# Holding every instruction behind the first group of products in the source's order on its engine

## The chip, the cores and the metric

The kernel runs on one core of a Trainium2 chip. The metric is the time of one execution on the device in microseconds (us), as the median of several runs.

## The reference: one layer of a hybrid decoder

The reference computes one inference step of one layer with three kinds of heads side by side: 6 mLSTM heads (A), 6 gated delta-rule heads (B) and 4 HGRN2 heads (C), each 128 wide. A prompt of 1024 tokens, with 16 learned meta tokens in front, and 8 short sequences of 8 tokens go through the same weights. Cut to what matters:

```python
h = _rmsnorm(x, norm_w)
proj = jnp.einsum('bld,de->ble', h, w_in)          # one combined projection, D_MODEL 2048
(aq, ak, av, ao, ai, af, bq, bk, bv, ba, bb, cq, cf, ci, z) = jnp.split(proj, SPLIT_POINTS, axis=-1)
...
for ls in seg_lens:                                 # the meta tokens, then the prompt
    o, st_a = _mlstm_segment(...)                   # gated linear attention with a running maximum
    o, st_b = _gdn_segment(...)                     # per chunk a triangular system is solved
    o, st_c = _hgrn_segment(...)                    # per-dimension decay
hcat = hcat * lax.rsqrt(jnp.mean(hcat * hcat, axis=-1, keepdims=True) + EPS)
y = hcat.reshape(bsz, L, MIX) * out_norm_w.astype(f32) * jax.nn.silu(z.astype(f32))
out = jnp.einsum('ble,ed->bld', y.astype(x.dtype), w_out)
return x + out, (st_a[0], st_a[1], st_a[2], st_b, new_conv, st_c)
```

A last RMS norm over `x + out` gives `y_prompt` and `y_sample`; the states of the heads after the prompt and after each short sequence are outputs too. All is in 32 bits.

## The kernel before

**Halves, heads and pieces.** The tokens are worked in two halves: the first holds the short sequences (64 columns), the meta tokens (16) and half of the prompt (512 columns), the second the other 512. In each half the columns of the combined projection are computed head by head, in groups; a head needs four or five tiles of 128 columns (`k`, `q`, `v`, `o`, `z` for A, `k`, `q`, `v`, `z` for B, `f`, `q`, `v`, `z` for C). Behind the second half comes the output projection, in units of 512 output columns: four units with five blocks of tokens each for the first half (the last four blocks are prompt rows, the first the short sequences), then five units for the second. An accumulator is a PSUM bank (`acc`, in the output `oacc`); there are eight banks in all, for these and for everything else that TensorE writes.

**The feed.** The projections go in 32 bits at full matmul speed by splitting: a weight piece of 512 rows by 128 columns, `wraw`, is loaded by a DMA on SP's queue; ScalarE makes its rounded high part `whi`, VectorE the rest `wlo = wraw - whi`; TensorE then multiplies high by high, high by low and low by high. Each of the three has four buffers. While TensorE works on piece p, `feed_ahead` splits piece p+3 and then issues the load of piece p+7. A piece has 24 products of 288 or 304 columns in the first half and 12 of 512 in the second.

**Scans beside the products.** The work of a head behind its tiles (its scan) is written as a Python generator; each `yield` ends a step. Four queues hold such generators: `scan`, `fin` (the norm and gate of a head's output, `finish`), `post` and `bg`. Behind each four or so products `weave.pump()` looks at the head of each queue and issues its next step, if the step is due. What is due comes from a model of the program itself: `Clock` keeps a time for each of TensorE, VectorE, ScalarE and GpSimd, adds a cost for each instruction that is issued, and a step's follower is due `LATENCY = 0.4` us behind the end of the last instruction of the step; a few steps add a hint of their own (`ck.last += 8.0` behind the substitution, `ck.last += 2.5` behind the loads of an A head). Each instruction goes through `Engine.__getattr__` (line 137 issues it, so nearly every compute instruction has that line in the profile); each DMA goes through `DMA`, SP's queue. At most two heads are open: `start_head` drains the older one, and at the units of the output `weave.drain_queue` drains a queue to its end.

**The order on the engines.** The program thus issues all instructions in one sequence, the source's order. Before this change that is only a priority: the build orders each engine's queue itself, and where by its own estimate an instruction's operands or buffers are not ready, a later one of the same engine that is ready goes ahead. The order so found is fixed at build time; the engine then runs its queue from front to back.

Names used below:

- A heads, `mlstm_scan`: `turn_in` loads the values (`v1`) and the output gate (`og`) in turned layout; then the gate of the 80 small rows (transpose `pot`, ScalarE's `t<-pot`), the gate of the prompt rows (`S.activation(og, og, ...)` twice, `s<-s` in the profile), and in the first half `meta_rows`, a ScalarE copy of the 16 meta rows (`meta`), which the product `pum` reads.
- B heads, `gdn_scan`: `Ball` is written out to DRAM (`db`) and read back as rows `Bb`; `substitute` solves blocks of 16 rows in 15 steps of two VectorE operations, `Yt<-Yc,Bb` and `Yc<-Yc,Yt`, then a product with a mask into `Y2` and a transpose into `X2` (`Y` and `X` in the profile), which the products `pz` read.
- C heads, `hgrn_scan`: seven levels, each with exponentials `Ex` on ScalarE, sums on VectorE, products `X` on GpSimd, and then scores `pa` on TensorE.
- `prep_B` (queue `bg`, begun in group 19 of the first half) prepares the second half's input: loads `px`, squares (`pxs`), transposes, and writes `hbhi` and `hblo`, which `load_hB` reads into `hB` when the second half starts.
- At the end of each output unit, for each block of tokens: a DMA loads the residual rows `res`, VectorE adds the accumulator to them (which frees the bank), ScalarE squares them (`oscr`), GpSimd multiplies by the last norm's weights `fnw`. At the end of the first unit the queues `scan` and `fin` are drained and four loads of `fnw` are issued before that. `finish` writes a turned copy (`yd`) to DRAM, loads it back (`s<-yd`), gates it and stores its high and low parts (`y<-zs`, `y<-y`), which `load_y` reads for the output products.

Of the kernel before, what the change touches and what calls it, by code (L numbers as in the profile page):

```python
# [48 lines left out]
class Half:  # L49
    def __init__(self, index):  # L50
        self.index = index
        self.first = index == 0
        self.width = WA if self.first else WB
        n0 = 1 if self.first else 0

        self.base = NT0 if self.first else 0
        self.tiles = ([(HALF, NT0)] if self.first else []) + [(P * c, P) for c in range(NC)]
        self.gtiles = ([(0, NT0)] if self.first else []) + [(self.base + P * c, P) for c in range(NC)]
        self.groups = ([Group(NT0, 1, HALF, 0, True)] if self.first else []) + [Group(P, NC, 0, n0, False)]
        self.ggroups = ([Group(NT0, 1, 0, 0, True)] if self.first else []) + [Group(P, NC, self.base, n0, False)]  # L60
        self.main, self.gmain = self.groups[-1], self.ggroups[-1]
# [24 lines left out]
class Clock:  # L86


    def __init__(self):
        self.t = {"T": 0.0, "V": 0.0, "S": 0.0, "G": 0.0}  # L90
        self.dep = self.last = 0.0

    def begin(self):
        self.dep = self.last = self.t["T"]
# [14 lines left out]
class Engine:  # L109
# [21 lines left out]
    def __getattr__(self, op):  # L131
        f = getattr(self.engine, op)

        def call(out, *a, **k):
            fast = self.name == "T" and op == "matmul" and a[0].dtype == F32R
            self.clock.run(self.name, self.cost(op, out, fast) + (1.2 if k.get("op") == ALU.pow else 0.0))
            return f(out, *a, **k)  # L137
        return call


class Stream:
    def __init__(self, gen, lag=None):
        self.gen, self.lag, self.due, self.done = gen, lag, 0.0, False

# [46 lines left out]
def hybrid_step(ctx, tc, i, o):  # L191
    nc = tc.nc
    ck = Clock()
    V, S, G, T = (Engine(ck, n, e) for n, e in (("V", nc.vector), ("S", nc.scalar), ("G", nc.gpsimd), ("T", nc.tensor)))
    DMA = nc.sync.dma_start
    weave = Weave(ck)

    cp = ctx.enter_context(tc.tile_pool(name="cp", bufs=1))
# [31 lines left out]
    def w_raw(col, g):  # L230
        raw = wp.tile([P, 512], F32, tag="wraw", name="wraw")
        v = raw.rearrange("p (k c) -> p k c", c=P)
        if col is None:
            V.memset(raw, 0.0)
            for src, at in ((C_AI, 0), (C_BB, 32), (C_AF, 64), (C_BA, 96)):
                DMA(v[:, :, at:at + HA], i["w_in"][0, 512 * g:512 * (g + 1), src:src + HA].rearrange("(k p) c -> p k c", p=P))
        else:
            DMA(v, i["w_in"][0, 512 * g:512 * (g + 1), col:col + P].rearrange("(k p) c -> p k c", p=P))
        return raw

    def o_raw(k, cg):
        raw = wp.tile([P, 512], F32, tag="wraw", name="wraw")
        DMA(raw, i["w_out"][0, P * k:P * (k + 1), 512 * cg:512 * (cg + 1)])
        return raw
# [49 lines left out]
    def run_group(half, cols, accs, parts, after=None):  # L294
        for g in range(NG):
            for n in range(len(cols)):
                whi, wlo = next_piece()
                for q in range(4):
                    k = 4 * g + q
                    cs = slice(P * q, P * (q + 1))  # L300
                    products = [(whi, 0, k == 0, False), (whi, 1, False, False), (wlo, 0, False, k == NK - 1)]
                    if cols[n] is None:
                        products = [(whi, 0, k == 0, False), (whi, 1, False, k == NK - 1)]
                    for w, part, first, last in products:
                        for a, off, cnt in accs[n][parts]:
                            T.matmul(a[:, 0:cnt], w[:, cs], hT[g][part][:, q, off:off + cnt], start=first, stop=last)
                    if q == 1:
                        feed_ahead()
                    weave.pump()
            if after:  # L310
                after(g)
# [50 lines left out]
    def load_nw(tile_, g):  # L362
        DMA(tile_, i["norm_w"][0:1, 512 * g:512 * (g + 1)].partition_broadcast(P))
        return tile_
# [4 lines left out]
    def load_x(n):  # L369
        xs = [row(("eghj" if n in (3, 4) else "abcd")[g], f"x{g}")[:, 0:512] for g in range(NG)]  # L370
        for g in range(NG):
            cs = slice(512 * g, 512 * (g + 1))
            if n:
                DMA(xs[g], i["x_prompt"][0, P * (n - 1):P * n, cs])
            else:
                DMA(xs[g][0:NSAMP], xs_flat[:, cs])
                DMA(xs[g][NSAMP:NT0], i["meta_tokens"][:, cs])
# [80 lines left out]
    first_accs = new_accs(halves[0], group_lists[0][0])  # L458
    run_group(halves[0], first_cols, first_accs, slice(0, 1))
    weave.drain_queue("bg")  # L460


    params = cp.tile([P, 92], F32, name="params")
# [1278 lines left out]
    for half in halves:  # L1742
        toks = []
        for n, (c0, cnt) in enumerate(half.tiles):
            if half.first and n == 0:
                toks.append((0, NSAMP, xs_flat, ys_flat))
            else:
                a = HALF * half.index + c0
# [85 lines left out]
```

## Time and profile before

| what | value |
|---|---|
| median of 3 runs | 2505.61 us (2505.42 to 2511.15) |
| profiled execution, its own time | 2506.0 us |
| its span | 2504.3 us |
| granted TensorE clock | 0.990 |
| instructions in the span | 43941 |
| TensorE busy | 2442.1 us, 98% |
| VectorE busy | 1425.5 us, 57% |
| ScalarE busy | 991.2 us, 40% |
| GpSimd busy | 554.8 us, 22% |
| moved by DMA | 350.82 MB, mean 140 GB/s |

The span runs from the first to the last instruction; the time of the execution has 1.7 us around it. In rows of the profile an instruction stands as output<-inputs by the program's names without numbers, so several tiles with one tag can share a name (`s`, `t`, `y`). PE is TensorE, PEld its weight loads, DVE is VectorE, ACT ScalarE, POOL GpSimd, and SPq the queue of DMA issues on SP. A row of the time line has the start, the duration, the engine, the line, the operation, output<-inputs, and in brackets the idle time of the engine before it with what ended it.

### The profile page before, as it was taken

Reading aid. Unit: us, or ns where it says so; the run is one execution under the profiler, and the core shown is the slowest. Engines: PE = TensorE matmul, PEld = TensorE weight load, DVE = VectorE, ACT = ScalarE, POOL = GpSimd, SP = SyncE. Lnnn points to the kernel's source line nnn. Section 1 sums busy time; section 2 is a strip of 40 time slices with the busy share of each in tenths; the row PEclk is TensorE's granted clock in tenths of the full one; section 3 lists DMA queues with packets and bytes.
Section 4 is the critical chain, followed back from the end, with each engine's and each line's share of the span. In section 5 each row is a group of like instructions: output and inputs, shape, how many; then the busy total and the mean of one; then the engine's idle time right before and its main releaser. Section 6 shows DMA issues by size and latency. Waiting matters only on the chain.

```text
span 2504.3 us, 43941 instructions
## 1 busy us (share of the span) xinstructions
PE 2442.1 (98%) x16032; PEld 2184.5 (87%) x16032; DVE 1425.5 (57%) x3080; ACT 991.2 (40%) x2430; POOL 554.8 (22%) x743
## 2 busy tenths in 40 slices
PE   6999999999999999999999999999999999999998
PEld 5898999999999999999787888888888888888886
DVE  7775655765656655556864556554654545323435
ACT  5643434443435333333642434333443334222324
POOL 5331212420313312113320113110320102211201
PEclk9999999999999999999999999999999999999999
DMA  5656665655645454447554455454554558636735
GB/s 129 152 140 147 147 146 133 162 131 130 158 99 138 99 131 118 118 119 203 132 132 115 120 123 136 122 130 101 138 127 114 129 123 257 183 84 200 254 97 185
DMA packets 681045, 350.82 MB, mean 140 GB/s; under 512 B 260004, under 2 KB 622076, under 8 KB 680828
## 3 DMA queue, kind: packets, MB, share of 16 engines
q1 hardware_dynamic: 680828, 348.01, 54.3%
q8 instruction: 126, 2.06, 0.4%
q14 instruction: 91, 0.75, 0.1%
HBM read 285.71 MB, written 62.19 MB: 139 GB/s over the span
## 4 chain that ended last, share of the span: by engine, by line
PE 80%; issue 5%; DVE 5%; DMA 4%; ACT 2%; POOL 2%; SPq 1%; POOLq 0%; DVEq 0%; ACTq 0%
PE acc L137 59%; PE oacc L137 9%; PE pa L137 1%; DVE wlo L137 1%; PE po L137 1%; PE nd L137 1%; PE pz L137 1%; PE pyy L137 1%; DMA wraw<-in_w_in_dram 1%; POOL res L137 1%; PE pu L137 1%; DMA px<-in_x_prompt_dram 1%; ACT whi L137 1%; PE poh L137 1%; PE pw L137 1%
## 5 line engine op out<-in xcount | busy, mean ns | idle before, releaser
L137 DVE TENSOR_TENSOR wlo<-wraw,whi 128x512 fp32r<-128x512 f32 x720 | 525.6, 734 | 569.6 <-ACT whi L137 552.1
L137 PE MATMUL acc<-hA,whi 128*128 128x288 f32 (+1 forms) x4544 | 826.2, 304 | 11.3 <-ACT whi L137 6.4
L137 ACT CAST whi<-wraw 128x512 fp32r<-128x512 f32 x720 | 441.9, 618 | 929.1 <-PE acc L137 641.2
L137 PE MATMUL acc<-hB,whi 128*128 128x512 f32 x2272 | 722.2, 400 | 4.3 <-ACT whi L137 2.1
L137 PEld LDWEIGHTS acc<-hA,whi 128*128 128x128 f32 x4544 | 679.6, 191 | 18.2 <-ACT whi L137 8.1
L137 PE MATMUL acc<-hA,wlo 128*128 128x288 f32 x2240 | 489.7, 299 | 1.6 <-DVE wlo L137 1.6
L137 PEld LDWEIGHTS acc<-hB,whi 128*128 128x128 f32 x2272 | 413.6, 189 | 86.2 <-ACT whi L137 2.7
L137 PE MATMUL acc<-hB,wlo 128*128 128x512 f32 x1120 | 441.1, 394 | 2.6 <-DVE wlo L137 2.6
L137 PEld LDWEIGHTS acc<-hA,wlo 128*128 128x128 f32 x2240 | 367.7, 190 | 2.7 <-DVE wlo L137 2.6
L137 PE MATMUL oacc<-whi,y 128*128 128x512 f32 x1088 | 343.4, 390 | 1.1 <-ACT whi L137 1.1
L137 PEld LDWEIGHTS acc<-hB,wlo 128*128 128x128 f32 x1120 | 211.0, 188 | 52.0 <-DVE wlo L137 6.8
L137 PEld LDWEIGHTS oacc<-whi,y 128*128 128x128 f32 x1088 | 204.2, 188 | 44.5 <-ACT whi L137 2.4
L137 PE MATMUL oacc<-wlo,y 128*128 128x512 f32 x576 | 224.8, 390 | 1.2 <-DVE wlo L137 1.2
L137 PEld LDWEIGHTS oacc<-wlo,y 128*128 128x128 f32 x576 | 108.1, 188 | 25.2 <-DVE wlo L137 3.1
L137 POOL TENSOR_TENSOR res<-res,fnw 128x512 f32<-128x512 f32 (+1 forms) x34 | 54.3, 1627 | 255.4 <-ACT oscr L137 255.4
L137 POOL TENSOR_TENSOR y<-y,zs 128x592 fp32r<-128x592 f32 (+1 forms) x32 | 46.0, 1437 | 171.4 <-ACT zs L137 106.7
L137 POOL TENSOR_TENSOR qd<-qT,emb 128x512 f32<-128x512 f32 x12 | 17.7, 1479 | 230.3 <-PE po L137 230.3
L137 DVE TENSOR_TENSOR Yt<-Yc,Bb 128x60 f32<-128x60 f32 (+8 forms) x180 | 37.6, 209 | 43.9 <-DMA Bb<-db 39.0
L137 POOL TENSOR_TENSOR hr<-hr,halfneg 128x4 f32<-128x4 f32 (+1 forms) x48 | 44.1, 919 | 61.1 <-DVE hr L137 58.4
L137 POOL TENSOR_TENSOR nrm<-nrm,halfneg 128x10 f32<-128x10 f32 x12 | 23.5, 1960 | 138.9 <-DVE nrm L137 138.9
L137 POOL TENSOR_TENSOR X<-Ex,hk 128x256 f32<-128x256 f32 (+1 forms) x40 | 39.1, 978 | 63.2 <-PE pa L137 41.8
L137 ACT ACTIVATE Wt<-pw,nrm 128x128 f32<-128x128 f32 (+1 forms) x54 | 19.8, 367 | 78.1 <-PE pw L137 78.1
(416 smaller groups left out, 2766.7 us busy)
## 6 DMA issues: line engine op xcount, KB each, us to landing
wraw<-in_w_in_dram SPq DMA_DIRECT2D x564, 256.0 KB
wraw<-in_w_out_dram SPq DMA_DIRECT2D x144, 256.0 KB
y<-y SPq DMA_DIRECT2D x16, 576.0 KB
px<-in_x_prompt_dram SPq DMA_DIRECT2D x32, 256.0 KB
yd<-y SPq DMA_DIRECT2D x128, 64.0 KB
out_dram<-sst SPq DMA_DIRECT2D x16, 512.0 KB
s<-yd SPq DMA_DIRECT2D x32, 256.0 KB
y<-zs SPq DMA_DIRECT2D x32, 256.0 KB
```

What stands on the lines that cost most here:

```text
L137: return f(out, *a, **k)
```

## The change

The instructions stay the same. `tc.keep_in_program_order` ties an instruction behind the one that was tied before it on the same engine: in order only, with no wait on its result. It is switched on behind the first group of products (once the background work of that stage is drained), and from there on it is called on each instruction that goes through `Engine` and on each DMA issue. What is issued before that point is ordered as it was.

```diff
@@ class Clock
         self.dep = self.last = 0.0
+        self.pin = None
@@ class Engine, __getattr__
-            return f(out, *a, **k)
+            ins = f(out, *a, **k)
+            if self.clock.pin:
+                self.clock.pin(ins)
+            return ins
@@ hybrid_step
-    DMA = nc.sync.dma_start
+
+    def DMA(*a):
+        ins = nc.sync.dma_start(*a)
+        if ck.pin:
+            ck.pin(ins)
+        return ins
+
@@ hybrid_step, behind the first group
     run_group(halves[0], first_cols, first_accs, slice(0, 1))
     weave.drain_queue("bg")
+
+    ck.pin = tc.keep_in_program_order
```

## The prediction

> **What bounds the kernel now.** I read the page first (busy shares, slices, chain, groups), then the busy time by stretches, then what TensorE waited for, and last the order of single instructions at the places where an engine's order differs from the source's.
>
> ```profile
> span 2504.3 us, 43941 instructions
> ...
> PE 2442.1 (98%) x16032; PEld 2184.5 (87%) x16032; DVE 1425.5 (57%) x3080; ACT 991.2 (40%) x2430; POOL 554.8 (22%) x743
> ...
> PE 80%; issue 5%; DVE 5%; DMA 4%; ACT 2%; POOL 2%; SPq 1%; POOLq 0%; DVEq 0%; ACTq 0%
> ...
> L137 ACT CAST whi<-wraw 128x512 fp32r<-128x512 f32 x720 | 441.9, 618 | 929.1 <-PE acc L137 641.2
> ...
> L137 DVE TENSOR_TENSOR Yt<-Yc,Bb 128x60 f32<-128x60 f32 (+8 forms) x180 | 37.6, 209 | 43.9 <-DMA Bb<-db 39.0
> ```
>
> TensorE (PE) is busy 2442.1 of 2504.3 us and makes 80% of the chain that ended last. The feed of the products is ahead of them: the high half of a weight piece, `whi`, sits idle 641.2 us for PE, that is, for one of its four buffers to come free. The order of the other engines therefore matters only where it makes PE late. How much is there to gain? The busy time by stretches says it (the first two numbers of a row are its length and PE's busy time):
>
> ```profile
> 62.00:122.00 60.00, 53.87 (x369) 51.32 (x370) 43.27 (x94) 42.11 (x84) 22.15 (x41) 0.97 0.65 150
> 122.00:643.00 521.00, 510.61 (x4190) 500.69 (x4191) 329.88 (x768) 208.14 (x577) 123.07 (x178) 0.98 0.61 142
> 643.00:1170.00 527.00, 525.96 (x4319) 516.35 (x4318) 313.37 (x754) 209.68 (x575) 129.56 (x176) 1.00 0.50 126
> 1170.00:1250.00 80.00, 72.51 (x383) 56.90 (x382) 58.57 (x107) 44.75 (x90) 25.25 (x28) 0.98 0.63 162
> 1250.00:2040.00 790.00, 787.28 (x4494) 651.80 (x4493) 440.77 (x941) 295.53 (x710) 136.95 (x156) 1.00 0.50 124
> 2040.00:2326.00 286.00, 285.65 (x1353) 237.77 (x1352) 115.16 (x198) 97.43 (x202) 58.91 (x51) 1.00 0.60 177
> 2326.00:2504.00 178.00, 165.89 (x723) 134.92 (x721) 74.97 (x120) 59.76 (x113) 26.85 (x21) 0.99 0.57 179
> ```
>
> PE's idle time in these seven rows is 6.1, 10.4, 1.0, 7.5, 2.7, 0.4 and 12.1 us, 40.2 us together. All of it lies behind the point from which the order is to be held, but for the first microseconds. The last 12 us are the end of the last unit of the output, whose order the change hardly touches. So about 28 us (1.1%) is the most that a better order can give, and there is no such bound on what a worse one can cost. What ended PE's waits:
>
> ```profile
> PE acc L137 <- ACT whi L137: 8.5, 9, 1.9
> PE pz L137 <- DVE Yc L137: 7.6, 3, 5.2
> ...
> PE pa L137 <- ACT U L137: 2.5, 1, 2.5
> PE pz L137 <- DVE X L137: 2.3, 1, 2.3
> ```
>
> **The change part by part.** Nothing is added to the work and no wait on a result: each instruction, and each issue on SP's queue, is tied behind the one that the program issued before it on the same engine. TensorE's own order is in the trace already that of the source at all but some hundred products, so it is held where it is; what changes is the order of VectorE, ScalarE, GpSimd and SP. Two things go: operations that ran ahead of their place, and the passing of an operation that waits. I price the places where either is seen.
>
> 1. Substitution of the B heads (12 of them, 15 steps `Yt`, `Yc` each on VectorE, from rows `Bb` that a DMA brings).
>
> ```profile
> 1606.38 1.92 SPq L1213 DMA_DIRECT2D Bb<-db  x3
> ...
> 1610.94 0.22 DVE L137 TENSOR_TENSOR Yt<-Yc,Bb 128x60 f32<-128x60 f32 x1 [4.27 <-DMA Bb<-db]
> ...
> 1611.34 0.68 DVE L137 TENSOR_TENSOR wlo<-wraw,whi 128x512 fp32r<-128x512 f32 x1
> ...
> 1614.48 0.69 DVE L137 TENSOR_TENSOR wlo<-wraw,whi 128x512 fp32r<-128x512 f32 x1
> ...
> 1617.71 0.69 DVE L137 TENSOR_TENSOR wlo<-wraw,whi 128x512 fp32r<-128x512 f32 x1
> ...
> 1619.86 0.31 DVE L137 STREAM_TRANSPOSE X<-Y 128x128 f32<-128x128 f32 x1
> 1620.17 1.28 DVE L137 TENSOR_TENSOR wlo<-wraw,whi 128x512 fp32r<-128x512 f32 x2
> ...
> 1616.64 0.39 PE L137 MATMUL acc<-hB,wlo 128*128 128x512 f32 x1
> ```
>
> SP ends its issue of `Bb` at 1608.3 and the first `Yt` starts at 1610.94: 2.64 us of landing. VectorE is idle then today as well (the page's 43.9 us before `Yt`, 39.0 of them for this DMA). But three `wlo` of 0.69 us are set into the chain behind it, and a fourth behind `Yc`. By the source the whole chain, `Yt` to the turn into `X`, comes first and these feeds after it. Without the three (0.68 + 0.69 + 0.69), `X` is ready 2.1 us sooner, at 1618.1 instead of 1620.17, and the first of the feeds, which PE reads at 1616.64, ends at 1618.8 rather than 1612.0: PE waits 2.2 us. Heads whose chain starts just behind a feed lose nothing, others up to the chain's 9 us less the feed's lead. I take 1.4 us, a little over half of the case shown, for all twelve: 17 us of loss. Against it stand PE's waits on `Yc` and `X`, 7.6 + 2.3 us in four pieces, of which the earlier `X` takes at most 2.1 us each, some 7. Net +10; ends -7 (no feed is late) and +26 (2.2 us for twelve, no gain).
>
> 2. A heads. In the first half the 16 meta rows are copied on ScalarE (`meta`) just ahead of the product `pum` that reads them.
>
> ```profile
> 273.84 1.28 ACT L137 ACTIVATE s<-s 128x512 f32<-128x512 f32 x2
> ...
> 284.67 0.30 ACT L137 COPY meta<-t 16x129 f32<-16x129 f32 x1
> ...
> 291.05 0.27 ACT L137 ACTIVATE t<-pot 80x128 f32<-80x128 f32 x1
> ...
> 288.56 0.27 PE L137 MATMUL pot<-ident,tho 128*80 128x128 f32 x1
> 288.67 0.40 PE L137 MATMUL pum<-meta,kwall 80*128 80x137 f32 x2
> ```
>
> Today the copy is done at 284.97 and the two big operations on the output gate (`s<-s`, 1.28 us) at 275.1, each long ahead. By the source ScalarE runs, after the transpose `pot` at 288.56: `t<-pot` 0.27, the two gate operations 1.28, the copy 0.30; only then can `pum`, which PE issues 0.11 us behind `pot`, start. That is 288.83 + 1.85 = 290.7 and some 0.2 for the hand-over, so PE stands 2.2 us. Six heads of the first half: 13 us. The loads for the gate and the values also ran ahead of their place by some 10 us; held, they still have about the 2.5 us that the source sets between, against 2.64 of landing above: 2 us for the other six. +15; ends 0 and +25 (landing of 4 us).
>
> 3. Output phase. Today the residual rows are loaded far ahead, and the last head is finished beside the next unit's products.
>
> ```profile
> 2131.66 1.05 SPq L1786 DMA_DIRECT2D res<-in_x_prompt_dram  x2
> ...
> 2166.85 0.38 SPq L814 DMA_DIRECT2D s<-yd  x1
> ...
> 2172.57 0.33 SPq L877 DMA_DIRECT2D y<-zs  x1
> 2173.99 0.33 SPq L877 DMA_DIRECT2D y<-y  x1
> ...
> 2160.44 0.68 DVE L137 TENSOR_TENSOR res<-res,oacc 64x512 f32<-64x512 f32 x1
> ...
> 2163.56 0.48 PE L137 MATMUL oacc<-whi,y 128*128 128x512 f32 x1
> ```
>
> The five loads for the first unit are issued around 2131.7, 30 us before the adds at 2160.44 that empty the accumulators. By the source they stand behind everything that finishes the last head: the turned load at 2166.85, two stores of `y` that wait for VectorE, ScalarE and GpSimd until 2174.3, four loads of the norm's weights. PE's next unit, at 2163.56, needs five accumulators and finds three free (eight banks, five per unit), so it can run 3 x 0.68 = 2.0 us. The fourth waits for an add: stores out at 2174.3, four loads at 0.42 and one at 0.5 to 2176.5, 2.64 of landing, 0.68 for the add, 2179.8: 14 us behind 2165.6. The chain may start up to some 2 us sooner with SP less loaded; I take 13. At the two next unit ends the loads stand behind the last weight load only, which is issued about one piece (3.2 us) before the end: 0.5 + 2.64 + 0.68 - 3.2 leaves about 0.6 of wait, hidden by the three free banks, but five loads follow one another at 0.5: 1.5 us each, 3. At the fourth unit the load of the next half's `y` stands between: 5. Sum +21; ends 0 (all landing in time) and +40.
>
> [...]
>
> 4. The turn from the first half to the second.
>
> ```profile
> 1179.29 2.35 PE L137 MATMUL acc<-hB,whi 128*128 128x512 f32 x9 [1.46 <-DMA hB<-hblo]
> ...
> 1186.35 2.10 PE L137 MATMUL pa<-X 128*128 128x128 f32 x18
> ```
>
> PE waits for the loads of `hB`, and at 1186.35 it fills the time with 18 products of the last C head (2.10 us). With C3's chain of levels in the source's order on three engines these may come later, and the drain of that head becomes serial: +5, ends -5 (feeds ahead of hoisted exponentials) and +14.
>
> 5. What goes. Early, ScalarE is caught behind operations that were set ahead of their place:
>
> ```profile
> 95.83 0.63 ACT L137 ACTIVATE pxs<-px 128x512 f32<-128x512 f32 x1 [2.63 <-DMA px<-in_x_prompt_dram]
> ...
> 99.89 0.63 ACT L137 ACTIVATE pxs<-px 128x512 f32<-128x512 f32 x1 [2.61 <-DMA px<-in_x_prompt_dram]
> ...
> 102.14 1.00 PE L137 MATMUL acc<-hA,whi 128*128 128x288 f32 x4 [1.85 <-ACT whi L137]
> ```
>
> Squares of `px`, background work whose place in the source is some 300 us later, held ScalarE 2.63 and 2.61 us for a DMA, and PE waited 1.85 us for `whi` at 102.14. Held in order this cannot happen: of the 6.1 us of the first stretch I take 6, and the 2.5 us of `pa` for `U` (a chain that ran late behind hoisted work). -9 with rounding; ends 0 and -18 (the like hidden in the 10.4 and 7.5 us).
>
> Sum: 10 + 15 + 21 + 5 - 9 = +42 on the profiled execution's 2506.0, 2548; that execution stands 0.4 above the median of 2505.61, which changes nothing at this size. The C heads' levels, which today run 20 to 30 us ahead of PE, come just in time; no row shows what that costs, it is bounded by nothing and some 20 us (twelve heads, 1.7 us each, the hand-overs of one level).
>
> **The rivals.** (a) Faster. The source's order is itself a plan: the program places each scan step when its clock model says that the operands are ready. If its lead times hold on the chip, items 1 to 4 cost a few microseconds and the hoists' damage is gone: 2506 - 9 - 7 and part of the rest of the 28 us, about 2487. For it speaks that every long PE wait in the trace is one behind passed or hoisted work; against it, that in the A heads the source leaves PE 0.11 us between `pot` and `pum`, and that the loads at a unit's end have no lead at all. It decides where the sum of 2 and 3 is under 15 us. (b) No change: PE's order is already the source's, feeds are three pieces (8 us and more) ahead, and stalls are taken up by that lead: within 7.5 us of 2506. Against it: accumulators have no such lead. (c) Much slower: SP is one queue for weights, turned loads and stores, and a store that waits for its producer holds the weight loads behind it. A weight load leads its use by about seven pieces less the wait for a buffer; where a hold is longer than some 10 us, PE stands. With 3 us at each of 30 heads this is +90 beside the forecast's, 2600 to 2640. [...]
>
> **How the numbers follow.** The forecast (2514 to 2595, sum 2548) gets 0.54, (a) 0.25, (b) 0.10, (c) 0.11. About 0.3%, 7.5 us, is what a measurement of this kernel can tell from no change. Slower is forecast and (c), 0.65; same 0.10; faster 0.25. The range goes down to 2484, which takes in most of (a), and up to 2600, the sum with the upper end of item 1 or 3 and the C levels' cost; some 0.15 to 0.2 is left out. The forecast's own range is 2514 to 2595.
>
> **What would show it.** In the profile after: `Yt` and `Yc` in one run without a `wlo` between, `wlo` among PE's waits near the B heads with about 17 us (item 1); PE's `pum` waiting on ScalarE's `meta` about 2 us at six heads (2); `oacc` waiting on VectorE's `res`, the longest near 13 us at the first unit's end, and the loads of `res` behind the stores of `y` (3); no square of `px` before about 360 us, and PE's busy time between 62 and 122 us close to its length of 60 us (5). The prediction is wrong on the fast side if PE's waits on `res` and `meta` are absent, on the slow side if `whi` waits for `wraw` DMAs in the middle of the kernel.

## Result: the held order takes 2671 us instead of 2506

The changed kernel takes 2671.24 us (median; 2667.91 to 2674.66), the kernel before in the same runs 2505.97 us. The ratio is 1.0657, with a 95% interval of 1.0638 to 1.0677. The direction was as forecast, and so were most of the places. The loss is 165 us where 42 were forecast; the time lies above the range's end of 2600, and above the 2640 of the slowest rival.

The page of the changed kernel (helper lines have moved by one, so compute instructions stand at L138, DMA issues at L203):

```profile
span 2667.1 us, 43721 instructions
...
PE 2479.7 (93%) x16032; PEld 2208.2 (83%) x16032; DVE 1434.9 (54%) x3080; ACT 990.1 (37%) x2428; POOL 530.9 (20%) x743
...
PE 67%; DVE 9%; DMA 8%; issue 6%; ACT 4%; SPq 3%; POOL 2%; DVEq 0%; ACTq 0%; POOLq 0%
...
L138 ACT CAST whi<-wraw 128x512 fp32r<-128x512 f32 x720 | 439.2, 619 | 724.9 <-PE acc L138 354.6
...
L138 DVE TENSOR_TENSOR Yt<-Yc,Bb 128x60 f32<-128x60 f32 (+8 forms) x180 | 36.7, 204 | 74.2 <-DMA Bb<-db 68.2
```

TensorE's share of the chain has fallen from 80 to 67%. Its idle time in the span (span less busy) is 187.4 us against 62.2 before: 125 us more. But its busy time has grown too, from 2442.1 to 2479.7 us, by 37.6 us for the same 16032 instructions. The two make the 163 us by which the span grew. The feed is no longer comfortably ahead: `whi` now waits for a buffer only 354.6 us in place of 641.2, and VectorE waits 68.2 us for `Bb`, where it waited 39.0.

What ended TensorE's waits behind the point where the hold begins (total us, times, longest us):

```profile
PE acc L138 <- DVE wlo L138: 45.0, 14, 11.4
PE oacc L138 <- ACT oscr L138: 28.4, 4, 15.7
PE pum L138 <- ACT meta L138: 17.9, 6, 4.9
PE pu L138 <- POOL vx L138: 12.3, 2, 7.3
PE oacc L138 <- ACT whi L138: 11.8, 3, 4.7
PE pa L138 <- POOL X L138: 8.8, 3, 4.3
PE pc L138 <- DVE st L138: 5.7, 2, 3.1
PE pu L138 <- DVE vx L138: 4.7, 3, 2.9
...
PE pz L138 <- DVE X L138: 0.4, 1, 0.4
```

Before, the largest of these was the first, with 4.2 us in total. The waits on `Yc` and `X` by the substitution's product, 9.9 us before, have gone, all but 0.4 us.

Three places, for each the chain of rows that makes TensorE wait. First a B head. SP's two issues, then VectorE, ScalarE and TensorE:

```profile
573.19 7.02 SPq L203 DMA_DIRECT2D db<-Ball  x8
581.44 1.89 SPq L203 DMA_DIRECT2D Bb<-db  x3
...
572.43 0.68 DVE L138 TENSOR_TENSOR wlo<-wraw,whi 128x512 fp32r<-128x512 f32 x1
...
585.46 0.24 DVE L138 TENSOR_TENSOR Yt<-Yc,Bb 128x75 f32<-128x75 f32 x1 [12.21 <-DMA Bb<-db]
...
593.07 0.31 DVE L138 STREAM_TRANSPOSE X<-Y 128x128 f32<-128x128 f32 x1
...
593.43 0.68 DVE L138 TENSOR_TENSOR wlo<-wraw,whi 128x512 fp32r<-128x512 f32 x1
...
572.37 0.62 ACT L138 CAST whi<-wraw 128x512 fp32r<-128x512 f32 x1 [4.14 <-issue]
594.76 0.62 ACT L138 CAST px<-xT 128x512 fp32r<-128x512 f32 x1 [21.77 <-DVE xT L138]
...
594.16 0.86 PE L138 MATMUL acc<-hA,wlo 128*128 128x288 f32 x2 [11.35 <-DVE wlo L138]
```

VectorE runs a `wlo` at 572.43 and next the first `Yt`, which must wait for `Bb` until 585.46: 12.2 us with nothing run, though one `wlo` could have been, since its `whi` was done at 572.99. The pieces behind that one are held on ScalarE: the next `whi` stands behind `px<-xT`, a rounding of the background preparation, which waits 21.77 us for VectorE's `xT`. On VectorE the 30 steps then run without a `wlo` between, as forecast, and the next `wlo` is at 593.43. TensorE, whose lead of some three pieces is used up, has stood 11.35 us. VectorE gets to `Yt` about when the first of the stores `db`, which must come ahead of `Bb`, is issued; about 2 us of the wait are that these stores took 7.0 us of SP's time (5.07 before at the head shown in the prediction).

Each of the twelve B heads has one such wait of TensorE. Ten are between 1.3 and 3.7 us, 24 us together. The other two, 11.35 and 7.59 us, are at the heads where VectorE waits longest for `Bb`: 12.21 and 8.92 us, against 3.5 to 6.2 us at the ten.

Then an A head, ScalarE and TensorE:

```profile
428.59 1.29 ACT L138 ACTIVATE s<-s 128x512 f32<-128x512 f32 x2 [2.88 <-DMA s<-tho]
429.91 0.30 ACT L138 COPY meta<-t 16x129 f32<-16x129 f32 x1
...
430.26 0.82 PE L138 MATMUL pum<-meta,kwall 80*128 80x137 f32 x2 [4.85 <-ACT meta L138]
```

The copy to `meta` stands behind the output gate's operations, and these wait 2.88 us for the gate's load (`s<-tho`), which runs no longer ahead. `pum` waits 4.85 us.

Last, the end of the first output unit, SP, VectorE and TensorE:

```profile
2274.28 0.33 SPq L203 DMA_DIRECT2D y<-zs  x1
2275.67 0.32 SPq L203 DMA_DIRECT2D y<-y  x1
2276.04 1.86 SPq L203 DMA_DIRECT2D fnw<-in_final_norm_w_dram  x4
2277.95 0.52 SPq L203 DMA_DIRECT2D res<-in_x_sample_dram  x1
...
2283.89 0.68 DVE L138 TENSOR_TENSOR res<-res,oacc 64x512 f32<-64x512 f32 x1 [10.29 <-DMA res<-in_x_sample_dram]
...
2269.14 0.40 PE L138 MATMUL oacc<-whi,y 128*128 128x512 f32 x1
2285.24 0.80 PE L138 MATMUL oacc<-whi,y 128*128 128x512 f32 x1 [15.71 <-ACT oscr L138]
```

The loads of `res` are issued behind the two stores of `y` and the four loads of the norm's weights, and the first lands 5.4 us after its issue ended (2278.47 to 2283.89). TensorE waits 15.7 us for the accumulators. The wait ends with ScalarE's `oscr`, which for the short sequences copies the second part of the accumulator and runs behind VectorE's add.

### The profile page after: what moved, and what is told of

Same layout as the page of the kernel before. It is cut to its first block, busy times and chain, and to the rows that moved or that the text cites. A ratio compares the mean times of both kernels' runs of the same rounds, so it can differ in the third digit from the quotient of the medians.

```text
span 2667.1 us, 43721 instructions
## 1 busy us (share of the span) xinstructions
PE 2479.7 (93%) x16032; PEld 2208.2 (83%) x16032; DVE 1434.9 (54%) x3080; ACT 990.1 (37%) x2428; POOL 530.9 (20%) x743
## 4 chain that ended last, share of the span: by engine, by line
PE 67%; DVE 9%; DMA 8%; issue 6%; ACT 4%; SPq 3%; POOL 2%; DVEq 0%; ACTq 0%; POOLq 0%
PE acc L138 45%; PE oacc L138 12%; SPq L203 3%; DVE wlo L138 2%; DMA Bb<-db 2%; DMA wraw<-in_w_in_dram 2%; DVE Yc L138 1%; DVE Yt L138 1%; PE pa L138 1%; PE nd L138 1%; DMA res<-in_x_prompt_dram 1%; PE po L138 1%; DMA db<-Ball 1%; PE pu L138 1%; ACT whi L138 1%
## 5 line engine op out<-in xcount | busy, mean ns | idle before, releaser
L138 PE MATMUL acc<-hA,whi 128*128 128x288 f32 (+1 forms) x4544 | 825.8, 304 | 7.2 <-DVE whi L138 4.7
L138 DVE TENSOR_TENSOR wlo<-wraw,whi 128x512 fp32r<-128x512 f32 x720 | 526.9, 739 | 478.8 <-ACT whi L138 460.9
L138 PE MATMUL acc<-hB,whi 128*128 128x512 f32 x2272 | 730.3, 404 | 0.7 <-ACT whi L138 0.7
L138 ACT CAST whi<-wraw 128x512 fp32r<-128x512 f32 x720 | 439.2, 619 | 724.9 <-PE acc L138 354.6
L138 PEld LDWEIGHTS acc<-hA,whi 128*128 128x128 f32 x4544 | 681.6, 191 | 12.7 <-ACT xscr L138 4.3
L138 PE MATMUL acc<-hA,wlo 128*128 128x288 f32 x2240 | 491.6, 300 | 24.2 <-DVE wlo L138 24.2
L138 PEld LDWEIGHTS acc<-hB,whi 128*128 128x128 f32 x2272 | 419.1, 192 | 83.6 <-ACT whi L138 1.1
L138 PE MATMUL acc<-hB,wlo 128*128 128x512 f32 x1120 | 444.4, 397 | 21.4 <-DVE wlo L138 21.4
L138 PEld LDWEIGHTS acc<-hA,wlo 128*128 128x128 f32 x2240 | 369.2, 191 | 26.3 <-DVE wlo L138 26.3
L138 PE MATMUL oacc<-whi,y 128*128 128x512 f32 x1088 | 352.9, 399 | 40.9 <-ACT oscr L138 28.4
L138 PEld LDWEIGHTS oacc<-whi,y 128*128 128x128 f32 x1088 | 209.4, 192 | 88.7 <-ACT oscr L138 30.1
L138 PEld LDWEIGHTS acc<-hB,wlo 128*128 128x128 f32 x1120 | 213.4, 191 | 71.8 <-DVE wlo L138 25.5
L138 PE MATMUL oacc<-wlo,y 128*128 128x512 f32 x576 | 228.9, 397 | 2.1 <-DVE wlo L138 2.1
L138 PEld LDWEIGHTS oacc<-wlo,y 128*128 128x128 f32 x576 | 110.7, 192 | 26.5 <-DVE wlo L138 3.9
L138 POOL TENSOR_TENSOR res<-res,fnw 128x512 f32<-128x512 f32 (+1 forms) x34 | 44.5, 1338 | 309.8 <-ACT oscr L138 309.6
L138 POOL TENSOR_TENSOR y<-y,zs 128x592 fp32r<-128x592 f32 (+1 forms) x32 | 46.0, 1439 | 298.0 <-ACT zs L138 244.5
L138 DVE TENSOR_TENSOR Yt<-Yc,Bb 128x60 f32<-128x60 f32 (+8 forms) x180 | 36.7, 204 | 74.2 <-DMA Bb<-db 68.2
L138 POOL TENSOR_TENSOR nrm<-nrm,halfneg 128x10 f32<-128x10 f32 x12 | 27.2, 2269 | 229.1 <-DVE nrm L138 229.1
L138 POOL TENSOR_TENSOR qd<-qT,emb 128x512 f32<-128x512 f32 x12 | 15.6, 1304 | 210.8 <-PE po L138 210.7
L138 POOL TENSOR_TENSOR X<-Ex,hk 128x256 f32<-128x256 f32 (+1 forms) x40 | 41.9, 1048 | 74.3 <-ACT Ex L138 74.2
L138 POOL TENSOR_TENSOR hr<-hr,halfneg 128x4 f32<-128x4 f32 (+1 forms) x48 | 47.4, 998 | 41.1 <-DVE hr L138 40.4
L138 DVE TENSOR_TENSOR res<-res,oacc 128x512 f32<-128x512 f32 (+1 forms) x36 | 23.5, 680 | 57.9 <-DMA res<-in_x_sample_dram 29.9
```

Source lines behind the costliest of these rows:

```text
L138: ins = f(out, *a, **k)
```

## Experiments

In all of them the order on an engine is held by the same call. One thing about it matters for the reading, and e9's rows below point to it: the call seems to tie an instruction behind the instruction issued just before it on its engine, whether that one is held or not (the section on the change says: behind the one that was tied before it; where all is held the two are the same). So where a single kind of work is held, that work can't pass anything issued ahead of it, while others can still pass it. The times are medians in us, the ratio is to the kernel before run beside it, with its 95% interval; "idle" is the span less TensorE's busy time, both of the one execution that was profiled.

| run | time | ratio | idle | TensorE busy |
|---|---|---|---|---|
| before (profile) | 2506.0 | | 62.2 | 2442.1 |
| changed kernel | 2671.2 | 1.0657 (1.0638 to 1.0677) | 187.4 | 2479.7 |
| e1 VectorE alone held | 2621.2 | 1.0460 (1.0429 to 1.0490) | 154.9 | 2467.1 |
| e2 ScalarE alone | 2579.1 | 1.0292 (1.0262 to 1.0322) | 118.4 | 2457.5 |
| e3 SP alone | 2588.3 | 1.0328 (1.0298 to 1.0358) | 129.5 | 2457.8 |
| e8 all but SP | 2629.6 | 1.0493 (1.0459 to 1.0527) | 157.5 | 2466.9 |
| e4 all, feed free | 2608.7 | 1.0412 (1.0382 to 1.0443) | 142.9 | 2463.2 |
| e5 all, meta copy ahead | 2645.0 | 1.0557 (1.0496 to 1.0618) | 173.0 | 2464.4 |
| e6 all, residual loads earlier | 2631.7 | 1.0504 (1.0466 to 1.0542) | 162.1 | 2464.9 |
| e7 the three together | 2573.1 | 1.0270 (1.0221 to 1.0320) | 117.1 | 2449.7 |
| e10 all, substitution later | 2685.0 | 1.0709 (1.0684 to 1.0734) | 198.3 | 2486.5 |
| e11 all, four places reordered | 2624.3 | 1.0467 (1.0438 to 1.0496) | 149.5 | 2468.5 |
| e9 feed and preparation alone | 2601.6 | 1.0375 (1.0353 to 1.0397) | 133.7 | 2470.5 |
| e12 preparation alone | 2558.4 | 1.0210 (1.0193 to 1.0228) | 106.0 | 2450.7 |
| e13 preparation alone, early, thin | 2528.5 | 1.0094 (1.0077 to 1.0112) | 84.2 | 2445.4 |
| e14 all, preparation early, thin | 2661.5 | 1.0632 (1.0603 to 1.0660) | 185.4 | 2478.8 |
| e15 all, all mends | 2576.2 | 1.0291 (1.0270 to 1.0312) | 119.7 | 2455.8 |

### Which engine's hold costs (e1, e2, e3, e8)

```diff
-            if self.clock.pin:
+            if self.clock.pin and self.name in ('V',):     # e1; e2: ('S',); e3: none; e8: all four
                 self.clock.pin(ins)
```

In e1, e2 and e8 the DMA issues are not held; in e3 they alone are.

> Only VectorE's instructions are held in the source's order; ScalarE, GpSimd, TensorE and SP's queue are ordered by the build as before. Theory 1 (an engine held in order keeps the feed's wlo behind an operation that waits): PE's waits on wlo near the B heads stay, some 30 to 45 us of the 45.5 seen with all held, and the lost clock with them: 2545 to 2570 us. Theory 2 (what costs is that SP's loads are issued later, so that data arrive late; the engines' own order is harmless): within 10 us of 2506.

> Only ScalarE's instructions are held. Theory 1: PE's waits of pum on the meta copy stay (18 us of idle PE in six pieces), nothing else of size: 2520 to 2545 us. Theory 2: within 10 us of 2506.

> Only SP's queue is held, all engines are ordered by the build as before. Theory 1: only the waits at the ends of the output's units stay, where the loads of res stand behind everything else (30 to 45 us of idle PE): 2535 to 2565 us. Theory 2: nearly the whole loss is there, 2640 to 2671 us.

> All four engines are held, SP's queue is ordered by the build as before. Theory 1: the waits at the ends of the output's units go, the others stay: 2600 to 2625 us. Theory 2: most of the loss goes, below 2530 us.

All three single holds cost more than theory 1 had for them: +115 us (39 to 64 expected), +73 (14 to 39) and +82 (29 to 59). Their sum, 270 us, exceeds what all cost together. All but SP costs +124, a little over theory 1's range. Theory 2 is out: with loads ordered by the build, three quarters of the loss is still there.

The traces show why the sum is too large. TensorE's idle time between 500 and 800 us is 2.6 us in the kernel before, 28.4 in the changed kernel, but 50.5, 38.1 and 53.5 us in e1, e2 and e3. That is half to three quarters of what each adds, and the sum counts it three times. Outside this stretch the three add 82 us of idle time together, the changed kernel 99. In e1 the products `pz` wait 15.7 us once in this stretch, in e3 `pum` waits 20.7 us once for a load of values; e12 below shows what sits there. What e1 to e3 lose outside it was not followed to a cause.

### Mending single places in the held kernel (e4, e5, e6, e7)

```diff
 # e4: the feed's splits are not held
             ck.begin()
+            held, ck.pin = ck.pin, None
             S.copy(hi, raw)
             ck.sync()
             V.tensor_tensor(lo, raw, hi, op=ALU.subtract)
+            ck.pin = held
 # e5: ahead of the output gate's operations
+        if half.first:
+            mrow = meta_rows(v1s[0][:, 0], P + 1)
 # e6: in the loop over the pieces of an output unit, not in the first one
+                if k == 7 and not (half.first and cg == 0):
+                    weave.drain_queue("post")
+                    early.update((n, res_load(half, cg, n, toks, nt)) for n in some)
```

> All held as in the changed kernel, but for the two operations of a weight piece's split (whi on ScalarE, wlo on VectorE), which the build may place. Theory 1 (the loss is a sum of places, each with its own late operation): PE's waits on wlo by the B heads, 47 us, go, and with each us of idle time some 0.27 us of slower clock (the first runs: PE's busy time grew by 25 us where its idle time grew by 93): 2671 - 60 = 2611 us. Theory 3 (holding part of an engine's order upsets the order that the build finds for the rest, so that freeing the feed only moves the waits): over 2640 us.

> All held; the copy of the 16 meta rows of an A head in the first half is issued ahead of the output gate's operations instead of behind them. Theory 1: the six waits of pum on meta, 18.0 us, go: 2671 - 23 = 2648 us. Theory 3: PE then waits for the next operation of the head by the same amount: above 2662 us.

> All held; the loads of the residual rows are issued at the eighth of the sixteen pieces of each output unit, not at its end, in every unit but the first of the first half. Theory 1: the waits of oacc on oscr but for the first (29.0 - 15.9) and on whi at the second half's units (12.3) and wlo there (3.3) go, 29 us: 2671 - 36 = 2635 us. Theory 3: above 2655 us.

> The three edits together (feed's splits free, meta copy ahead, residual loads earlier). Theory 1: the gains add, 60 + 23 + 36: 2671 - 119 = 2552 us; what is left over the kernel before is the first output unit's end (15.9), the C heads' chains and vx at drained heads. Theory 3: under 60 us of gain, over 2610 us.

The times of theory 1 hold to within 4 us for the three single edits: 2608.7 (2611 expected), 2645.0 (2648), 2631.7 (2635). The 62 us that freeing the feed gives back are the largest gain. In part that agreement is luck. In e4 the waits of the projections on `wlo` go, as expected, and `oacc`'s waits on `whi` go too (11.8 to 0.3 us), which the forecast didn't count; against them stands a new wait of `pz` for VectorE, 13.9 us in two pieces. At the B head shown above nothing is gained: TensorE waits 13.0 us there, now in `pz` for the end of the chain.

Together the three give 98 of 119 us. Part of what lacks is that e4 and e6 both reduce the same waits of `oacc` on `whi` (in e6 11.8 to 5.4 us), which can be gained only once. The wait of `pz` is there as in e4 (14.9 us).

### The wait for Bb or the length of the chain (e10, e11)

```diff
-        ready = ck.t["T"] + 7.0
+        ready = ck.t["T"] + 12.0
```

> All held; the step of the substitution is planned 12.0 us of the plan's time behind the issue of its rows Bb instead of 7.0, so that the source places it some 5 us later. Theory 1a (the feed is held by VectorE's wait for the DMA of Bb, 68 us in 12 pieces, more than by the chain itself): VectorE's wait falls under 30 us, PE's waits on wlo from 47 to under 20: 2671 - 35 = 2636 us. Theory 1b (the chain of 30 operations, some 8 us in one piece, holds the feed): PE's waits on wlo stay above 40 us, over 2660 us.

> All held, nothing free; the source's order is mended at four places: meta copy ahead, residual loads earlier, the substitution planned at 12.0 us, and at the end of the first output unit the adds that empty the accumulators stand before the drain of the last head and the loads of the norm's weights. Theory 1: 23 + 36 + 35 and 20 for the first unit's end (15.9 us and its clock): 2671 - 114 = 2557 us. Theory 3 (waits move elsewhere): over 2600 us.

e11 has e5's and e6's edits too, and empties the first unit's accumulators ahead of the drain. In e10 VectorE's wait for `Bb` falls from 68.2 to 21.1 us, TensorE's waits on `wlo` fall, but others grow:

```profile
PE oacc L138 <- ACT oscr L138: 29.1, 4, 15.7
PE acc L138 <- DVE wlo L138: 26.7, 10, 5.1
PE pu L138 <- POOL vx L138: 17.9, 7, 6.9
```

Of the 45 us on `wlo`, some 18 were thus due to the wait for `Bb`. The 27 left, 2.2 us a head, belong to the chain that no feed can enter and to the 21.1 us of waiting for `Bb` that remain. Yet the kernel got slower. `pu` waits more on `vx`, 17.9 us in place of 12.3 on GpSimd's and 9.9 in place of 4.7 on VectorE's, and `pum` waits 9.8 us for loads of values where it waited for none before this edit. That these come from heads which end 5 us later and so are drained later is likely, but not shown. So theories 1a and 1b each had a part, and the forecast of the time (2636) was wrong by 49 us. e11 gains 47 of 114 us and lies where theory 3 had it; e10's edit, which was to give 35 us of this, cost 14 by itself.

### Holding single work (e9, e12, e13, e14) and all mends (e15)

```diff
 # e12: hold only the background preparation, compute only; e9: the feed's splits too
+        held, self.clock.held = self.clock.held, s.hold       # in Weave.step
...
-            if self.clock.pin:
+            if self.clock.pin and self.clock.held:
...
+                weave.add("bg", prep_B()).hold = True
 # e13, e14: its place and pace
-            if half.first and n == 19:
+            if half.first and n == 4:
...
-            ck.last = ck.t["T"] + 6.0
+            ck.last = ck.t["T"] + 16.0
```

> The build orders everything but two things: the feed's splits and the preparation of the second half's input are held in the source's order among themselves, so that no square of px can pass a whi. Theory 1: PE's waits on whi and wlo between 62 and 122 us (6 us, and their clock) go, nothing is added: 2506 - 7 = 2499 us. Theory 3 (a partial hold upsets the rest of the build's order): slower than before by 10 us and more.

e9 took 2601.6 us. Its expectation described the hold wrongly: by these rows the feed was held not only against the preparation but against whatever came before it on the engine. What it shows is therefore another thing, VectorE's rows at a B head of the second half:

```profile
1689.64 0.22 DVE L139 TENSOR_TENSOR Yt<-Yc,Bb 128x60 f32<-128x60 f32 x1 [5.07 <-DMA Bb<-db]
...
1697.35 0.31 DVE L139 STREAM_TRANSPOSE X<-Y 128x128 f32<-128x128 f32 x1
1697.58 2.46 DVE L139 TENSOR_TENSOR wlo<-wraw,whi 128x512 fp32r<-128x512 f32 x4
```

The chain's own operations are not held here, only the splits and the preparation, and still four `wlo` stand behind the whole chain, 8 us, just as in the changed kernel. A hold on the splits suffices to take away what the build did best: to put `wlo` into the chain. e9 and e12, which follows, differ in this hold alone, and by 43 us.

> Only the preparation of the second half's input is held, on all its engines but SP; the feed is free. In the run that held the feed too, each held instruction was tied behind the instruction issued just before it on its engine, whichever that was, so that a wlo could not pass the substitution: its 41 us of waits on wlo and 29 on X came from the feed's hold. Theory 1 (it is the hold of the feed that costs; the squares of px running ahead cost some 6 us early): 2506 - 7 = 2499 us, PE's waits on whi between 62 and 122 us gone, no wait of PE on wlo over 2 us. Theory 3 (any hold upsets the build's order elsewhere): 2520 us and more.

It took 2558.4 us, 59 us over theory 1. The stretch from 500 to 800 us in the kernel before (length, busy time of TensorE), and then in e12, with e12's longest waits of TensorE:

```profile
500.00:800.00 300.00, 297.37 (x2474) 291.18 (x2473) 175.54 (x443) 122.67 (x346) 60.06 (x91) 0.98 0.54 127
```

```profile
500.00:800.00 300.00, 249.26 (x1995) 241.31 (x1994) 162.53 (x389) 93.52 (x272) 46.95 (x73) 0.90 0.57 130
...
PE acc L139 <- ACT whi L139: 19.7, 10, 7.6
PE pum L139 <- DMA s<-vT: 18.9, 1, 18.9
PE pz L139 <- DVE Yc L139: 17.1, 3, 13.0
```

TensorE's idle time has grown by 48 us there, which is more than in the whole span (44 us): between 62 and 300 us it fell from 13.9 to 8.0 us, about the early gain that theory 1 had. In the kernel before the preparation's squares are done by 131 us and its stores spread from 138 to 677 us; held at its place in the source, it squares from 360 us on and stores from 462 to 780 us. At the wait of 18.9 us one can see what this does, on SP, ScalarE and TensorE:

```profile
636.67 1.80 SPq L207 DMA_DIRECT2D wraw<-in_w_in_dram  x2
653.67 1.96 SPq L207 DMA_DIRECT2D hbhi<-px  x4
...
664.04 0.56 SPq L207 DMA_DIRECT2D s<-vT  x1
...
653.04 0.60 ACT L139 CAST px<-xT 128x512 fp32r<-128x512 f32 x1
...
667.17 2.06 PE L139 MATMUL pum<-s,kwall 128*128 128x129 f32 x8 [18.86 <-DMA s<-vT]
```

SP issues nothing from 638.5 to 653.7, 15.2 us: a store of the preparation, `hbhi`, stands at the head of its queue and waits for `px`, which ScalarE rounds only at 653.04. The load `s<-vT` that `pum` needs comes behind it. This is what the prediction's rival (c) describes. SP's waits for `px` between 500 and 800 us sum to 61.3 us here and to 0.8 us in the kernel before; in e1, e2 and e3 they are 55.3, 35.0 and 56.6 us, and in e1 the queue stands 15.6 us for the same store. So the single holds seem to meet the same obstacle, though only in e12 was it moved away. In the changed kernel the sum is 29.8 us. e13 and e14 move the place of the preparation in the source.

> As the run that holds only the preparation of the second half's input (2558 us, 48 us of PE's idle time between 500 and 800 us), but the source begins that preparation in group 4 instead of 19 and plans its second part at 16 us a step instead of 6, as thinly as it ran in the kernel before. Theory 4 (the preparation's place costs: run where the source has it, its loads and 128 stores meet the heads of 500 to 800 us): that idle time goes to under 10 us, 2500 to 2515 us. Theory 3 (any hold upsets the build's order, wherever the held work stands): 2540 us and more, with waits at other places.

> As the changed kernel, all held, with the preparation begun in group 4 and planned thinly in the same way. Theory 4: PE's idle time between 500 and 800 us, 28 us in the changed kernel, falls by half or more, and some clock with it: 2671 - 20 to 35 = 2636 to 2651 us. Theory 3: within 10 us of 2671.

> All mends together in the held kernel: feed's splits free, meta copy ahead, residual loads earlier, adds of the first output unit ahead of the drain, preparation begun in group 4 and thin. Theory 1 with 4: from the 2573 us of the three mends, 20 for the first unit's end and 20 to 30 for the preparation: 2520 to 2535 us. Theory 3: above 2550 us.

e13, 300 to 500 and 500 to 800 us:

```profile
300.00:500.00 200.00, 192.44 (x1540) 188.86 (x1539) 120.19 (x273) 79.31 (x205) 43.39 (x62) 0.98 0.61 147
500.00:800.00 300.00, 285.20 (x2358) 279.20 (x2357) 172.31 (x418) 110.21 (x316) 55.67 (x87) 0.96 0.52 125
```

TensorE's idle time between 500 and 800 us falls from 51 to 15 us, SP's waits for `px` there from 61.3 to 3.3 us, and the time from 2558 to 2528. More than half of e12's loss was thus the place and pace of that work, as theory 4 says, but its forecast (under 10 us, 2500 to 2515 us) was missed: some 24 us are left, with 7.6 us of idle time now between 300 and 500. In the fully held kernel (e14) the same move brings only 10 us, which is theory 3's figure: the idle time falls from 28.4 to 19.6 us between 500 and 800, and grows from 12.1 to 19.0 us between 62 and 300. With all mends (e15, 2576.2, on theory 3's side) nothing is gained over e7's three: the first unit's end waits 4.2 us instead of 14.2, but `pu` waits 26.1 us on GpSimd's `vx` instead of 13.6.

No version run here beats the kernel before; the nearest, e13, is 0.9% slower.

## Why the prediction was wrong

**Right.** The direction; that VectorE runs the substitution in one piece with `wlo` behind it; that `pum` waits on `meta` at six heads (17.9 us against 13 forecast); that `oacc` waits at the units' ends, longest at the first (15.7 against 13), though by the profile ScalarE's `oscr` ends the wait and not VectorE's `res`; that no square of `px` runs before 360 us (the first is at 372); that the waits of `pz` go. Rivals (a) and (b) fail by the same rows. The sign named for rival (c) did appear: between 122 and 2040 us ScalarE's `whi` waited 81.8 us in 30 pieces for `wraw`, 15.1 us in 8 before. But in the changed kernel it hardly reached TensorE, whose projections wait 1.4 us on `whi` behind the start of the hold. It reached TensorE in e12, where a hold of 15.2 us was followed by a wait of 18.86; the rival's limit of some 10 us was the author's estimate.

**Item 1, +10 forecast, the step that failed most.** The mechanism was right, its size was not. The step took VectorE's idle time before `Yt` as unchanged (it is idle "today as well") and priced only the three `wlo` inside the chain. But in the kernel before, a split that becomes ready can go ahead of a `Yt` that waits; held, it stands behind it, and VectorE gets to `Yt` sooner: it waits 68.2 us for `Bb` in place of 39.0. TensorE waited 45.0 us on `wlo` (17 forecast); less the 9.9 us of `pz`, the item is about +35, above its upper end of 26. The two heads with the longest waits for `Bb` make 18.9 us of it. e4 gives 62 us back, clock and some other waits included, and e10 shows the two parts, wait and chain.

**Item 2, +15:** 17.9 us. Four heads are at 1.9 to 2.4 us, as the 2.2 forecast; two are at 4.7 and 4.9, where the gate's load lands late (2.88 us at 430 us). That late landing was forecast for the second half, where it doesn't show. No run shows the 0.2 us taken for the hand-over: at 430 us `meta` ends at 430.21 and `pum` starts at 430.26, and `t<-pot` starts 0.04 us behind the end of `pot` (425.40 to 425.44).

**Item 3, +21:** 28.4 (`oscr`) and 11.8 (`whi`), 2.1 (`wlo`): 42 us. At the first unit two steps failed: that the loads land in 2.64 us (the first took 5.4 us behind four other loads), and that TensorE still fills three accumulators (it ran 0.9 us, the products of one, and not 2.0). What the item left out are the second half's units, 13.9 us, where ScalarE waits in order for the same loads with `whi` behind it.

**Item 4 and the C levels, +5 and 0 to 20:** at the turn (1200 to 1325 us) TensorE is idle for 25.4 us, against 7.5 before (1150 to 1275): +18, beyond the item's end of 14. It waits there on GpSimd's `X` and `vx` (7.7 and 5.0) and on VectorE's `st` and `vx` (3.1 and 2.9). Waits of these kinds elsewhere make some 13 us. The prediction's bound for the C levels counts twelve heads; there are eight, four in each half, and no run shows the 1.7 us it takes for each.

**Item 5, -9:** TensorE's idle time between 62 and 122 us fell from 6.1 to 3.9 us only. The step that squares done at their place cost nothing failed: e12, which holds the preparation alone, gains 5.9 us before 300 us, and has 48 us more of idle time between 500 and 800 us, where its stores hold SP's queue. How much of this is in the changed kernel's loss is small by e14 (10 us).

**Left out altogether:** TensorE's clock. Idle time was priced at its own length, with no reason given; the 125 us more of it came with 37.6 us more busy time. It is described below. The added waits of items 1 to 4, some 126 us by the numbers above, are about the 125 us of added idle time.

What stays open: what e1 to e3 lose outside the stretch from 500 to 800 us, why e13 still loses 24 us, and what makes up the 68 us that e7 still loses, beyond the waits named.

## What to carry to other kernels

An order that the build finds for an idle-looking engine can be worth a good deal (165 us here with all held, 115 with VectorE alone): price a hold by the ready work that stands behind the operation that waits, not by the engine's idle time in the profile of before. The same holds for a queue of DMA issues: in e12 a store that waited for its data held the loads behind it for 15 us. A feed that every product needs should not share an in-order queue with a long chain whose input a DMA brings (here TensorE waited 45.0 us on `wlo`), or must be written into its gaps in the source (this second way was not run here). And the waits of TensorE cost more than their length in these runs (0.14 to 0.4 us of added busy time for each us of added idle time), so that a sum of waits has to be raised for the clock.

## What the runs showed of the hardware

The granted clock fell after many of TensorE's waits, though not after all. Around the 11.35 us wait shown above, in the changed kernel (a row has the stretch, its length, TensorE's busy time with the number of products, the granted clock, then the share and GB/s of the DMA):

```profile
582.00:594.00 12.00, 0.81 (x6) 0.66 0.44 117
594.00:598.00 4.00, 3.84 (x15) 0.50 0.59 117
598.00:602.00 4.00, 4.00 (x51) 0.82 0.76 138
602.00:606.00 4.00, 4.00 (x68) 1.00 1.00 258
```

In the four microseconds behind the wait the granted clock is 0.50, in the next four 0.82 on average, then 1.00. A wait of 2.02 us, which ended at 1827.87, was followed by a lower clock too, 0.59 and 0.56 for two microseconds each:

```profile
1823.87:1827.87 4.00, 1.98 (x10) 1.00 0.42 105
1827.87:1829.87 2.00, 2.00 (x5) 0.59 0.39 89
1829.87:1831.87 2.00, 2.00 (x7) 0.56 1.10 305
1831.87:1833.87 2.00, 2.00 (x10) 1.00 0.51 133
```

Of twelve of this trace's waits between 1.1 and 2.8 us, seven (1.9 to 2.8 us) were followed within 4 us by two microseconds at a clock of 0.56 or less, five (1.1, 1.3, 1.8, 1.9 and 2.4 us) by a clock that stayed at 1.00. So among these the length of a wait alone doesn't tell whether the clock falls. Over the runs of the table, each us of added idle time comes with 0.14 to 0.4 us of added busy time, 0.30 in the changed kernel.

What stands ahead of the prediction as full matmul speed is, in the kernel before and at a granted clock of 1.00, one product of 512 columns of the split pieces every 0.227 us (15 begin from 1500.35 to 1503.75), 0.44 ns a column. Products of 32-bit operands that are not split, `pum<-s,kwall` with 129 columns, begin every 0.10 us there (eight from 1496.51 to 1497.32), 0.79 ns a column. No run has the projections without the split, so what it saves on them is not shown.
